# Half of the gate projections made between the attention blocks and kept in DRAM, and eight modulation chunks moved from the merge to the MLP

## The chip, the cores and the metric

The kernel runs on one core of one Trainium2 chip. The time is that of one execution on the device, in microseconds; of runs of one kernel the median is taken. Profiles are of one execution. A core has TensorE (matrix products, in the profile PE, its weight loads PEld), VectorE (DVE), ScalarE (ACT), GpSimd (POOL) and SyncE (SP, which here only issues DMAs).

## The reference

Two layers of a trunk are run over 640 tokens: 512 latent ones and 128 of context. Cut to what matters here, a layer is

```python
h = modulate(rms_norm(x, g_attn), sh1, sc1)          # sh1 ... gt2: six pieces of silu(c) @ w_mod + b_mod
cb, cc, cv, gq, gk, gv, nq, nk, nv, mq, mkv, mkr, gates = in_project(h, w_in)
y_conv, y_gqa, y_na, y_mla = ...                     # a short convolution and three kinds of attention
g1, g2, g3, g4 = split(sigmoid(gates), 4)            # each 1024 wide
merged = (g1 * (y_conv @ w_branch_conv) + g2 * (y_gqa @ w_branch_gqa)
          + g3 * (y_na @ w_branch_na) + g4 * (y_mla @ w_branch_mla))
x = x + gt1 * (merged @ w_o)
x = x + gt2 * (square(relu(modulate(rms_norm(x, g_mlp), sh2, sc2) @ w_ff1)) @ w_ff2)
```

The `gates` depend on `h` alone, not on the attention. `c` is one vector for the latent tokens and another for the context tokens, so the modulation is 6 x 1024 columns for each of two vectors.

## The kernel before

Activations lie with their features on the partitions: a chunk is 128 features x 640 tokens, two halves of 320. A weight slab is 128 output columns with all its row chunks, mostly 8: 128 x 1024 numbers, 512 KB. For precision each operand is split into a high and a low part in fp32r (`prefetch`, `split`): ScalarE casts the high part, VectorE subtracts it to get the low part. A product is then three matmuls per row chunk (`steps`, L199 to L201: high x high, high x low, low x high), and a slab of 8 row chunks is 48 matmuls of 320 columns, 24 per half. One such group of three is called a step.

`plan` lists all slabs in the order of use (`feed`). `take` hands out the next one and, through `look`, splits the following one meanwhile. A large slab (tag `w`) has two buffers for the raw weights and two for each part. A small slab (tag `b`: the branch projections `wb` of 2 or 4 row chunks, and the MLA heads' second projections) has one of each, and `look` never splits one small slab while another is being used:

```python
            if last == "b" and (self.raws[0][3] if self.raws else self.feed[0][3]) == "b":
                return
```

A layer has three stages.

*Mixers* (`mixers`, `attend`). 16 heads of 5 blocks each (four of latent queries, one of context queries) go through a software pipeline: scores on TensorE, minimum on VectorE, exponential on ScalarE, a factor on GpSimd, transposition on TensorE (L538), split, product with the values. 8 heads are of windowed attention (GQA), 4 of neighbourhood attention, 4 of latent attention (MLA). Between the parts of a block `fill` runs steps of the remaining projections on TensorE: a list of tasks in a fixed order, with a budget per block (`RATE`, in units in which a step is 410). A task may wait until so many heads have begun or ended (`wait`); `fill` then returns with nothing done, whatever stands behind that task, and its budget adds up. TensorE's order is the program's; the order on the other engines in this stage is a scheduler's. Two banks of PSUM are there for projections.

*Merge* (`merge`). For each of eight output columns j and each of the four branches: the gate's slab (`wg`, large) times `h`, the branch's small slab (`wb`) times the branch's output, tanh of the gate on ScalarE (L889), the product (L891, L893) on VectorE, the sum over branches on GpSimd. At the end of a column `mh` and `ml` are the split sum (L902, L903). A column is 252 matmuls. From here to the end of the MLP the order of every engine is that of the program, SP's too. In layer 0's merge 32 modulation chunks are made beside it (`mod_chunk`): a chunk is 128 columns of the modulation, one DMA of 512 KB into `wm`, which has one buffer, and two passes of VectorE over it (L253), one for each vector. There are five places for chunks in each column from the second on.

*MLP* (`mlp`, `boundary`). Up and down projections in four quarters, each slab large. In layer 0 the 48 chunks of the next layer's modulation are made there, one per slab in 54 places; what is left would be made in one piece before the last `boundary`.

Of the kernel before, what the change touches and what calls it, by code (L numbers as in the profile page):

```python
# [17 lines left out]
P = 128  # L18
D = 1024
KC = D // P  # L20
DEPTH = 2
# [18 lines left out]
HEAD = 100  # L40
FILL_SLABS = (GQ + 1, GQ + 2, CONV + 2, CONV + 4, CONV, GQ + 3, NQC, NK, NV, MKV, NQC + 1, NK + 1, NV + 1,
              MQ, MQ + 1, MKR, HEAD, HEAD + 1, CONV + 3, HEAD + 2, CONV + 5, HEAD + 3, CONV + 1)
# gate, first row chunk and number of chunks of its branch's projection; first chunk of y
BRANCHES = ((1, 0, 4), (2, 4, 2), (0, 8, 2), (3, 6, 2))
Y_OF = {0: 0, 1: 2, 2: 6, 3: 8}
# [20 lines left out]
class Net:  # L66
    def __init__(self, ctx, nc, tc, t):
# [7 lines left out]
        self.ydram = [self.dr.tile([10, P, NTOK], F32, name=f"ydram{l}") for l in range(DEPTH)]  # L75
        self.xdram = self.dr.tile([P, KC, NTOK], F32, name="xdram")
# [19 lines left out]
    def psum(self, n1, n2=0):  # L96
        """PSUM for one phase: n1 single banks, n2 pairs of banks"""
# [18 lines left out]
    def plan(self, l):  # L116
        t, f = self.t, self.feed
        wa = lambda c: f.append((t["wa"][l, c], KC, P, "w", True))
        for c in (GK, GQ, GV) + FILL_SLABS:
            if c == MKR:  # L120
                f.append((t["wkr"][l], KC, 32, "w", True))
            elif c >= HEAD:
                f.append((t["wmla"][l, c - HEAD], 1, 384, "b", True))
            else:
                wa(c)
        for j in range(KC):
            for g, c0, n in BRANCHES:
                f.append((t["wg"][l, j, g], KC, P, "w", False))
# [11 lines left out]
    def raw(self):  # L140
        """start the load of the next slab"""
# [5 lines left out]
    def prefetch(self, dst=None):  # L147
        """split the next slab; start the load of the one after it"""
# [9 lines left out]
        if eng and kc == KC:  # L158
            # in halves, so that no engine is held for long
# [1373 lines left out]
```

## Time and profile before

| | |
|---|---|
| time, three runs | 2405.25, 2408.97, 2410.58 us (median 2408.97) |
| profiled execution | span 2405.3 us from the first to the last instruction |
| TensorE | busy 2315.2 us (96%), mean granted clock 0.987 |
| VectorE, ScalarE, GpSimd | 1404.0, 935.7, 367.3 us (58, 39, 15%) |
| DMA | 242.96 MB, 101 GB/s in the mean |
| mixers of layer 0, layer 1 | 84.4 to 405.2, 1261.3 to 1579.0 us |
| first merge, its eight columns | 405.2 to 701.2 us |

Busy time is the union of an engine's instructions. A matmul is shown with some 310 ns though 1012 of them start in 148 us: each is pipelined into the next, so TensorE's busy share says that it was never left waiting for long, not that it ran at its peak. The start of one block and the start of the next tell more.

### The profile page before, as it was taken

Reading aid. Unit: us, or ns where it says so; the run is one execution under the profiler, and the core shown is the slowest. Engines: PE = TensorE matmul, PEld = TensorE weight load, DVE = VectorE, ACT = ScalarE, POOL = GpSimd, SP = SyncE. Lnnn points to the kernel's source line nnn. Section 1 sums busy time; section 2 is a strip of 40 time slices with the busy share of each in tenths; the row PEclk is TensorE's granted clock in tenths of the full one; section 3 lists DMA queues with packets and bytes.
Section 4 is the critical chain, followed back from the end, with each engine's and each line's share of the span. In section 5 each row is a group of like instructions: output and inputs, shape, how many; then the busy total and the mean of one; then the engine's idle time right before and its main releaser. Section 6 shows DMA issues by size and latency. Waiting matters only on the chain. (4 is left out here: it accounts for less than half of the span.)

```text
span 2405.3 us, 39685 instructions
## 1 busy us (share of the span) xinstructions
PE 2315.2 (96%) x15766; PEld 2251.6 (94%) x15766; DVE 1404.0 (58%) x2744; ACT 935.7 (39%) x1877; POOL 367.3 (15%) x468
## 2 busy tenths in 40 slices
PE   8899888999999999999999998999999999999998
PEld 4899888999999999999988997899999999999998
DVE  5776676666645777776467767753333454343433
ACT  5555554322224332222255656542222343131311
POOL 0333321111111000000123333211111200000001
PEclk9999999999999999999999999999999999999999
DMA  6323312444431344443331231042222212222222
GB/s 231 96 72 86 91 35 102 167 142 148 151 114 59 132 158 157 147 153 123 97 124 58 83 112 38 25 162 73 82 71 86 90 45 72 78 76 75 79 80 71
DMA packets 85321, 242.96 MB, mean 101 GB/s; under 512 B 9744, under 2 KB 31248, under 8 KB 83728
## 3 DMA queue, kind: packets, MB, share of 16 engines
q1 hardware_dynamic: 85136, 240.43, 30.9%
q8 instruction: 124, 2.03, 0.3%
q14 instruction: 61, 0.50, 0.1%
HBM read 222.14 MB, written 12.75 MB: 98 GB/s over the span
## 5 line engine op out<-in xcount | busy, mean ns | idle before, releaser
L199 PE MATMUL pr<-hhi,whiw 128*128 128x320 f32 (+1 forms) x2752 | 868.4, 316 | 20.5 <-ACT st L300 9.6
L201 PE MATMUL pr<-hhi,wlow 128*128 128x320 f32 (+1 forms) x2752 | 852.7, 310 | 2.3 <-DVE wlow L166 1.4
L200 PE MATMUL pr<-hlo,whiw 128*128 128x320 f32 (+1 forms) x2752 | 853.4, 310 | 0.1
L199 PEld LDWEIGHTS pr<-hhi,whiw 128*128 128x128 f32 (+1 forms) x2752 | 516.4, 188 | 26.9 <-ACT st L300 11.7
L201 PEld LDWEIGHTS pr<-hhi,wlow 128*128 128x128 f32 (+1 forms) x2752 | 515.6, 187 | 5.0 <-DVE wlow L166 2.6
L200 PEld LDWEIGHTS pr<-hlo,whiw 128*128 128x128 f32 (+1 forms) x2752 | 516.7, 188 | 3.4 <-DVE hlo L1159 2.6
L165 ACT CAST whiw<-raww 128x1024 fp32r<-128x1024 f32 x184 | 192.7, 1047 | 286.6 <-PE pr L200 269.4
L166 DVE TENSOR_TENSOR wlow<-raww,whiw 128x1024 fp32r<-128x1024 f32 x184 | 237.1, 1289 | 60.8 <-ACT whiw L165 60.3
L199 PE MATMUL pr<-hh,whiw 128*128 128x320 f32 x832 | 257.0, 309 | 0.0
L200 PE MATMUL pr<-hl,whiw 128*128 128x320 f32 x832 | 256.9, 309 | 0.0
L201 PE MATMUL pr<-hh,wlow 128*128 128x320 f32 x832 | 256.9, 309 | 0.0
L253 DVE SCALAR_TENSOR_TENSOR junk<-wm,cb 128x1024 bf16<-128x1024 f32 x160 | 195.7, 1223 | 46.8 <-DMA wm<-in_wm 43.9
L916 DVE SCALAR_TENSOR_TENSOR x<-pr,mod,x 128x256 f32<-128x256 f32 x320 | 107.7, 379 | 195.1 <-PE pr L201 192.9
L1114 POOL TENSOR_TENSOR sqs<-sqs,sq 128x320 f32<-128x320 f32 x48 | 47.7, 993 | 969.8 <-ACT sq L1112 941.9
L529 POOL TENSOR_SCALAR p<-p,sm 128x512 f32<-128x512 f32 (+3 forms) x160 | 123.2, 771 | 369.5 <-DVE sm L528 299.6
L894 POOL TENSOR_TENSOR acc<-acc,sg 128x320 f32<-128x320 f32 x96 | 89.0, 931 | 521.1 <-DVE sg L893 521.0
L524 ACT ACTIVATE p<-S,sm 128x641 f32<-128x641 f32 (+6 forms) x160 | 112.1, 701 | 139.0 <-DVE sm L515 65.1
L889 ACT ACTIVATE sg<-pr 128x320 f32<-128x320 f32 x128 | 55.5, 437 | 284.1 <-PE pr L201 276.3
L200 PEld LDWEIGHTS pr<-hl,whiw 128*128 128x128 f32 x832 | 156.4, 188 | 0.0
L199 PEld LDWEIGHTS pr<-hh,whiw 128*128 128x128 f32 x832 | 156.4, 188 | 0.0
L201 PEld LDWEIGHTS pr<-hh,wlow 128*128 128x128 f32 x832 | 156.4, 188 | 0.0
L893 DVE SCALAR_TENSOR_TENSOR sg<-sg,pr 128x320 f32<-128x320 f32 x96 | 46.2, 487 | 187.4 <-PE pr L201 187.4
(207 smaller groups left out, 3774.5 us busy)
## 6 DMA issues: line engine op xcount, KB each, us to landing
raww<-in_w SPq DMA_DIRECT2D x128, 512.0 KB, 3.6
wm<-in_wm SPq DMA_DIRECT2D x80, 512.0 KB, 3.7
raww<-in_wg SPq DMA_DIRECT2D x64, 512.0 KB, 3.8
raww<-in_wa SPq DMA_DIRECT2D x42, 512.0 KB, 3.6
wm<-in_wm SPq DMA_DIRECT2D x8, 1024.0 KB, 14.3
raww<-in_wo SPq DMA_DIRECT2D x16, 512.0 KB, 3.6
rawb<-in_wb SPq DMA_DIRECT2D x48, 128.0 KB, 2.1
kt<-kt SPq DMA_DIRECT2D x24, 224.0 KB, 3.2
```

The source lines that it names most:

```text
L165: nc.scalar.copy(hi, raw)
L166: nc.vector.tensor_tensor(lo, raw, _r(hi), ALU.subtract)
L199: nc.tensor.matmul(out, lhsT=whi[:, kw, :], rhs=xhi[:, kx, sl], start=(i == 0), stop=False)
L200: nc.tensor.matmul(out, lhsT=whi[:, kw, :], rhs=xlo[:, kx, sl], start=False, stop=False)
L201: nc.tensor.matmul(out, lhsT=wlo[:, kw, :], rhs=xhi[:, kx, sl], start=False, stop=(i == n - 1))
L253: nc.vector.scalar_tensor_tensor(self.junk, raw, 1.0, self.cb[v], ALU.mult, ALU.mult, accum_out=self.mod[l]["mod"][:, v, i:i + 1])
L524: nc.scalar.activation(p[:, :B["n"]], B["sc"], AF.Exp, bias=sm[:, 0:1], scale=-1.0, accum_out=sm[:, 1:2])
L529: nc.gpsimd.tensor_scalar(p[:, :n], p[:, :n], sm[:, 1:2], 1.0, ALU.mult, ALU.mult)
L889: nc.scalar.activation(sg, gp[hf][:, :HALF], AF.Tanh, scale=0.5)
L894: nc.gpsimd.tensor_tensor(a, a, sg, ALU.add)
L916: self.nc.vector.scalar_tensor_tensor(x[:, j, o + a:o + b], ps[:, a:b], m[:, v, g0 + j:g0 + j + 1], x[:, j, o + a:o + b], ALU.mult, ALU.add)
L1114: eng.tensor_tensor(self.acc[h], self.acc[h], sq, ALU.add)
```

## The change

Sixteen of the 32 gate slabs of a layer, those of columns 4 to 7 (`EARLY`), are made in the mixers, as sixteen more fill tasks between the others (`None` in the table `FILL`, of which two of its eight lines are shown). Each passes its tanh through a tile `gt` to DRAM (`gdram`). The budgets per block are raised. In the merge, columns 4 to 7 have only the branches' small slabs; the tanh values come back by DMA, four tiles at the end of column 2 into the last chunks of `mh` and `ml`, twelve into the tiles of `h` once the last gate of column 3 has been made. Layer 0's merge makes 24 chunks, two per branch in columns 1 to 3, and the other eight stand at the head of the MLP's list.

```diff
+EARLY = tuple(range(4, KC))
+EARLY_GATES = tuple((j, b[0]) for j in EARLY for b in BRANCHES)
+FILL = (("q1", (GQ + 1,)), ("q2", (GQ + 2,)), None, ("c0", (CONV + 2, CONV + 4, CONV)), ("q3", (GQ + 3,)), None,
+        ("nq0", (NQC,)), None, ("nk0", (NK,)), ("nv0", (NV,)), None, ("ckv", (MKV,)), None, ("nq1", (NQC + 1,)),
...
-RATE = (2000, 2200, 2000)
+RATE = (3500, 3700, 3500)
...
+    def early_gate(self, l, n):
+        w = self.take()
+        t = self.at.tile([P, NTOK], F32, name="gt", tag="gt", bufs=1)
+        for h in range(2):
+            ps = self.bank()
+            yield from self.steps(ps[:, :HALF], w, self.h, hsl(h))
+            self.nc.scalar.activation(t[:, hsl(h)], ps[:, :HALF], AF.Tanh, scale=0.5)
+        self.nc.sync.dma_start(self.gdram[l][n], t)
...
     def merge(self, l, x):
-        self.mod_todo = deque([(0, i) for i in range(16, 48)] if l == 0 else [])
+        self.mod_todo = deque([(0, i) for i in range(16, 40)] if l == 0 else [])
...
             for j in range(KC):
                 for i, (g, c0, n) in enumerate(BRANCHES):
-                    w = self.take()
-                    if j:
-                        self.mod_chunk()
-                    gp = [self.half(w, h, hf) for hf in range(2)]
+                    if j not in EARLY:
+                        w = self.take()
+                        if j:
+                            self.mod_chunk()
+                            self.mod_load()
+                        gp = [self.half(w, h, hf) for hf in range(2)]
+                        if (j, i) == (EARLY[0] - 1, len(BRANCHES) - 1):
+                            for name in ("hhi", "hlo"):
+                                u = self.hp.tile([P, KC, NTOK], F32R, name=name, tag=name)
+                                early.extend(_r(u[:, k]) for k in range(KC))
+                            gates(4, len(EARLY_GATES))
...
                     w = self.take()
-                    if j and i == 0:
-                        self.mod_load()
-                        self.mod_chunk()
...
                     for hf in range(2):
...
+                        if j in EARLY:
+                            tg = early[(j - EARLY[0]) * len(BRANCHES) + i][:, hsl(hf)]
+                        else:
+                            tg = sg
+                            nc.scalar.activation(sg, gp[hf][:, :HALF], AF.Tanh, scale=0.5)
...
-                    if j:
+                    if j and j not in EARLY:
+                        self.mod_chunk()
                         self.mod_load()
...
     def mlp(self, l, x, first):
-        self.mod_todo = deque([(l + 1, i) for i in range(48)] if l + 1 < DEPTH else [])
+        self.mod_todo = deque([(0, i) for i in range(40, 48)] + [(1, i) for i in range(48)] if l == 0 else [])
```

Three places where the order of instructions changes. In these rows `S` is a pair of PSUM banks, `pr` one bank, `hhi` and `hlo` the two parts of `h`, `whiw` and `wlow` those of a large slab, `whib` and `wlob` those of a small one.

TensorE in layer 0's mixers, the seventh head's second block, before: from one transposition of probabilities (L538) to the next.

```order
L538 MATMUL S_2209<-ident,p 128x128 x5
L199 MATMUL pr<-hhi,whiw 128x320
L200 MATMUL pr<-hlo,whiw 128x320
L201 MATMUL pr<-hhi,wlow 128x320
...
L479 MATMUL S_2228<-kt,qt 128x128
L480 MATMUL S_2228<-kt,qt 128x128
...
L538 MATMUL S_2246<-ident,p 128x128 x5
```

The same place now (lines are shifted by 15).

```order
L553 MATMUL S_2659<-ident,p 128x128 x5
L494 MATMUL S_2666<-kt,qt 128x128
L495 MATMUL S_2666<-kt,qt 128x128
L570 MATMUL pr<-pt,vt 128x128 x2
L553 MATMUL S_2686<-ident,p 128x128 x5
```

Where five steps stood between two transpositions, none stands now. In the blocks before it there are 8 or 9 steps instead of 5, and in the neighbourhood heads' second block 76 in one piece.

VectorE in layer 0's merge, the second branch of a column, before: the low parts of a small and a large slab, a chunk (`junk`, two passes), the branch's product (`sg`).

```order
L166 TENSOR_TENSOR wlob<-rawb,whib 128x256 [waits DMAHW1_49,Activation_49]
L166 TENSOR_TENSOR wlow<-raww,whiw 128x1024 [waits DMAHW2_49,Activation_49]
L253 SCALAR_TENSOR_TENSOR junk,mod_106<-wm,cb_4589 128x1024 [waits DMAHW4_49,DVE_49]
L253 SCALAR_TENSOR_TENSOR junk,mod_106<-wm,cb_4590 128x1024 [waits DVE_49]
L893 SCALAR_TENSOR_TENSOR sg<-sg,pr 128x320 [waits PE_49,Activation_49] x2
L166 TENSOR_TENSOR wlob<-rawb,whib 128x256 [waits DMAHW5_49,Activation_49]
```

A branch of columns 1 to 3 now.

```order
L181 TENSOR_TENSOR wlob<-rawb,whib 128x256 [waits DMAHW4_49,Activation_49]
L181 TENSOR_TENSOR wlow<-raww,whiw 128x1024 [waits DMAHW5_49,Activation_49]
L268 SCALAR_TENSOR_TENSOR junk,mod_108<-wm,cb_5583 128x1024 [waits DMAHW7_49,DVE_49]
L268 SCALAR_TENSOR_TENSOR junk,mod_108<-wm,cb_5584 128x1024 [waits DVE_49]
L941 SCALAR_TENSOR_TENSOR sg<-sg,pr 128x320 [waits PE_49,Activation_49] x2
L268 SCALAR_TENSOR_TENSOR junk,mod_108<-wm,cb_5583 128x1024 [waits DMAHW2_49,DVE_49]
L268 SCALAR_TENSOR_TENSOR junk,mod_108<-wm,cb_5584 128x1024 [waits DVE_49]
L181 TENSOR_TENSOR wlob<-rawb,whib 128x256 [waits DMAHW0_49,Activation_49]
```

A second chunk stands behind the product, ahead of the next branch's low parts.

VectorE in the merge's columns 4 to 7, now, from the end of column 5 on: the split sum (`ml`), then low parts of small slabs and products by turns, each product with a gate from `hhi`.

```order
L954 SCALAR_TENSOR_TENSOR ml<-acc,mh 128x640 [waits Activation_49]
L181 TENSOR_TENSOR wlob<-rawb,whib 128x512 [waits DMAHW0_49,Activation_49]
L939 SCALAR_TENSOR_TENSOR acc<-hhi,pr 128x320 [waits PE_49] x2
L181 TENSOR_TENSOR wlob<-rawb,whib 128x256 [waits DMAHW1_49,Activation_49]
L941 SCALAR_TENSOR_TENSOR sg<-hhi,pr 128x320 [waits PE_49] x2
```

Before, a large slab's low part and a chunk stood between a small slab's low part and its product, and the next small slab's low part came behind the next gate's slab. Now each small slab's low part stands directly behind the product of the small slab before it.

## Rows read from the trace of the kernel before

**Rows 1.** Windows; columns: stretch, PE, PEld, DVE, ACT, POOL busy (x instructions), PEclk, DMA, GB/s
```profile
84.39:405.21 320.82, 291.40 (x2045) 275.45 (x2043) 234.35 (x533) 185.29 (x438) 103.57 (x151) 0.97 0.20 60
405.21:553.20 147.99, 146.42 (x987) 144.88 (x988) 94.65 (x151) 46.33 (x82) 20.45 (x22) 1.00 0.54 178
553.20:701.20 148.00, 148.00 (x1012) 148.00 (x1011) 89.44 (x136) 39.00 (x68) 22.18 (x24) 1.00 0.44 139
701.20:1237.40 536.20, 533.89 (x3639) 530.94 (x3638) 354.75 (x667) 177.72 (x309) 29.36 (x28) 1.00 0.37 125
1261.33:1579.00 317.67, 290.49 (x2045) 274.30 (x2042) 234.00 (x532) 185.72 (x438) 103.70 (x151) 0.97 0.20 61
```

**Rows 2.** Timeline of PE, block starts; columns: start, us, engine, line, operation, tiles, count
```profile
159.19 0.63 PE L538 MATMUL S<-ident,p 128*128 128x128 f32 x4 [0.99 <-DVE pt L545]
...
167.56 0.71 PE L538 MATMUL S<-ident,p 128*128 128x128 f32 x5
...
177.90 0.49 PE L538 MATMUL S<-ident,p 128*128 128x128 f32 x3
...
183.79 0.38 PE L538 MATMUL S<-ident,p 128*128 128x128 f32 x2
```

**Rows 3.** Timeline of PE, blocks at the end of the first mixers
```profile
392.61 0.82 PE L538 MATMUL S<-ident,p 128*128 128x128 f32 x6
...
397.99 1.06 PE L538 MATMUL S<-ident,p 128*128 128x128 f32 x6 [1.32 <-issue]
```

**Rows 4.** Windows of 10 us in the first mixers and merge
```profile
290.00:300.00 10.00, 6.34 (x42) 4.95 (x40) 9.29 (x19) 5.93 (x16) 5.77 (x14) 1.00 0.01 2
340.00:350.00 10.00, 8.86 (x46) 8.44 (x47) 6.56 (x12) 4.74 (x10) 2.05 (x2) 0.66 0.00 0
410.00:420.00 10.00, 9.10 (x59) 8.35 (x58) 5.53 (x8) 5.86 (x10) 0.00 (x0) 1.00 1.04 393
```

**Rows 5.** Timeline of DVE, first chunks of the first merge
```profile
453.33 1.22 DVE L253 SCALAR_TENSOR_TENSOR junk<-wm,cb 128x1024 bf16<-128x1024 f32 x1
...
459.54 1.23 DVE L253 SCALAR_TENSOR_TENSOR junk<-wm,cb 128x1024 bf16<-128x1024 f32 x1 [3.72 <-DMA wm<-in_wm]
...
471.94 1.23 DVE L253 SCALAR_TENSOR_TENSOR junk<-wm,cb 128x1024 bf16<-128x1024 f32 x1 [0.22 <-DMA wm<-in_wm]
```

**Rows 6.** Timeline of DVE at the end of a merge column
```profile
482.67 0.49 DVE L893 SCALAR_TENSOR_TENSOR sg<-sg,pr 128x320 f32<-128x320 f32 x1 [0.39 <-PE pr L201]
484.92 0.82 DVE L903 SCALAR_TENSOR_TENSOR ml<-acc,mh 128x640 fp32r<-128x640 f32 x1 [1.75 <-ACT mh L902]
485.66 0.69 DVE L166 TENSOR_TENSOR wlob<-rawb,whib 128x512 fp32r<-128x512 f32 x1
```

**Rows 7.** Lines by form, first merge: columns as the page's part 5
```profile
L889 ACT ACTIVATE sg<-pr 128x320 f32<-128x320 f32 x63 | 27.3, 437 | 133.8 <-PE pr L201 126.0 <-DVE acc L891 7.5 <-POOL acc L894 0.3
...
L165 ACT CAST whib<-rawb 128x256 fp32r<-128x256 f32 x24 | 9.7, 406 | 44.4 <-PE pr L200 38.9 <-DMA rawb<-in_wb 5.5
...
L166 DVE TENSOR_TENSOR wlob<-rawb,whib 128x256 fp32r<-128x256 f32 x24 | 13.9, 577 | 0.0
```

**Rows 8.** DMA issues, whole run: out<-in, engine, count, KB, us to landing
```profile
rawb<-in_wb SPq DMA_DIRECT2D x48, 128.0 KB, 2.1
...
rawb<-in_wb SPq DMA_DIRECT2D x16, 256.0 KB, 2.7
```

**Rows 9.** DMA issues from 405.8 to 416.7 us
```profile
x<-ydram SPq DMA_DIRECT2D x8, 320.0 KB, 6.9
...
rawb<-in_wb SPq DMA_DIRECT2D x1, 128.0 KB, 6.3
```

**Rows 10.** Timeline of DVE around the last MLP boundary of layer 0
```profile
1163.29 0.68 DVE L916 SCALAR_TENSOR_TENSOR x<-pr,mod,x 128x256 f32<-128x256 f32 x2 [2.84 <-PE pr L201]
...
1164.48 1.22 DVE L166 TENSOR_TENSOR wlow<-raww,whiw 128x1024 fp32r<-128x1024 f32 x1
```

More of the change, by code (lines that the diff above doesn't have):

```diff
@@ L75, in __init__ @@
         self.ydram = [self.dr.tile([10, P, NTOK], F32, name=f"ydram{l}") for l in range(DEPTH)]
+        self.gdram = [self.dr.tile([len(EARLY_GATES), P, NTOK], F32, name=f"gdram{l}") for l in range(DEPTH)]
         self.xdram = self.dr.tile([P, KC, NTOK], F32, name="xdram")
@@ L118, in plan @@
         wa = lambda c: f.append((t["wa"][l, c], KC, P, "w", True))
-        for c in (GK, GQ, GV) + FILL_SLABS:
-            if c == MKR:
+        gates = iter(EARLY_GATES)
+        slabs = [GK, GQ, GV]
+        for task in FILL:
+            slabs += task[1] if task else [GATE]
+        for c in slabs:
+            if c == GATE:
+                f.append((t["wg"][l][next(gates)], KC, P, "w", True))
+            elif c == MKR:
                 f.append((t["wkr"][l], KC, 32, "w", True))
@@ L711, in part @@
                     yield ns
-            tasks = [gqa_q(1), gqa_q(2), ("c0", (ns for ns in self.conv(l, 0) if ns >= 0)), gqa_q(3),
-                     na_q(0), na_k(0), na_v(0), ("ckv", M.keys()), na_q(1), na_k(1), na_v(1), ("mq", M.queries()),
-                     ("kr", M.rotary()), ("m0", M.prep(0)), ("m1", M.prep(1)), ("c1", part()), ("m2", M.prep(2)),
-                     ("c2", part()), ("m3", M.prep(3)), ("c3", part())]
+            gen = {"c0": (ns for ns in self.conv(l, 0) if ns >= 0), "ckv": M.keys(), "mq": M.queries(), "kr": M.rotary()}
+            gen.update(gqa_q(c) for c in (1, 2, 3))
+            for c in range(2):
+                gen.update((na_q(c), na_k(c), na_v(c)))
+            gen.update((f"m{hd}", M.prep(hd)) for hd in range(4))
+            gen.update((f"c{i}", part()) for i in (1, 2, 3))
+            gates = iter(range(len(EARLY_GATES)))
+            tasks = []
+            for task in FILL:
+                if task:
+                    tasks.append((task[0], gen[task[0]]))
+                else:
+                    n = next(gates)
+                    tasks.append((f"g{n}", self.early_gate(l, n)))
+            assert next(gates, None) is None
             names = [n for n, _ in tasks]
@@ L855, in merge, with gates @@
             order = [Y_OF[g] + q for g, _, n in BRANCHES for q in range(n)]
-            raw = {}
-            for i, c in enumerate(order):
-                raw[c] = x[:, i] if i < KC else yp.tile([P, NTOK], F32, name="acc", tag="acc", bufs=3)
-                if i < BRANCHES[0][2]:
-                    nc.sync.dma_start(raw[c], self.ydram[l][c])
+            raw = {c: x[:, i] if i < KC else _r((mh, ml)[i - KC][:, KC - 1]) for i, c in enumerate(order)}
+            for c in order[:BRANCHES[0][2]]:
+                nc.sync.dma_start(raw[c], self.ydram[l][c])
+            early = deque(_r(a[:, k]) for k in (KC - 1, KC - 2) for a in (mh, ml))
+            def gates(a, b):
+                for n in range(a, b):
+                    nc.sync.dma_start(early[n], self.gdram[l][n])
             for j in range(KC):
-                acc = None
+                acc = yp.tile([P, NTOK], F32, name="acc", tag="acc", bufs=3)
                 for i, (g, c0, n) in enumerate(BRANCHES):
-                    w = self.take()
-                    if j:
-                        self.mod_chunk()
-                    gp = [self.half(w, h, hf) for hf in range(2)]
                     yc = Y_OF[g]
+                    if j not in EARLY:
+                        w = self.take()
[8 more added lines that the diff above has]
+                            gates(4, len(EARLY_GATES))
                     for q in range(n if j == 0 else 0):
                         self.split(yh[:, yc + q], yl[:, yc + q], raw[yc + q])
-                    if acc is None:
-                        acc = yp.tile([P, NTOK], F32, name="acc", tag="acc", bufs=3)
                     w = self.take()
-                    if j and i == 0:
-                        self.mod_load()
-                        self.mod_chunk()
                     if (j, i) == (0, 0):
@@ L901, in merge @@
                             self.silu(yp, a, D)
+                elif j == EARLY[0] - 2:
+                    gates(0, 4)
                 nc.scalar.activation(mh[:, j], acc, AF.Copy, scale=0.5)
@@ L906, in merge @@
                 self.mod_chunk()
-            self.mod_done(0, 16, 48)
+            self.mod_done(0, 16, 40)
         wop = s.enter_context(tc.tile_pool(name="wop", bufs=1, side="right", reuse_waits="tile"))
@@ L995, in mlp @@
             up(q)
+            if l == 0 and q == 1:
+                self.mod_done(0, 40, 48)
             down(q - 1)
```

19 lines of the change are left out of this document (11 added, 8 removed).

## The prediction

> **What bounds the kernel now.** I read the windows by stage first, then block starts on TensorE inside the mixers, then VectorE and the DMA issues in the merge, because the change takes from one stage and gives to the other. The windows [rows 1] show the split. In the first merge TensorE is busy for 146.4 us of 148.0 and then for all of 148.0; 1012 matmuls in 148.0 us are 146 ns each, and I take that as the pace of a 128x320 matmul. The MLP is the same: 533.9 of 536.2. So there a stage costs its matmuls. The mixers are another matter: 29.4 of 320.8 us idle in layer 0, 27.2 of 317.7 in layer 1. The busy count flatters them, as a matmul's tail covers short gaps. The starts of the blocks show what is lost [rows 2]: the fifth head takes 18.71 us (159.19 to 177.90) with 22 fill steps, while the five blocks from 167.56 to 183.79 take 16.23 with 21 steps, without a gap. A step is three matmuls, 0.44 us, so a dense head is 7.0 us of attention plus its steps, and the fifth head loses 18.71 - 7.0 - 9.7 = 2.0 us. Added up over all 79 block starts of a layer, against the dense pace, it is 47 us; 94 us for both layers is the most that better filling could give.
>
> **The change, part by part.** The matmuls are the same, 14,382 rows on TensorE in both. Per layer 16 gate slabs of 48 matmuls, 16 x 48 x 0.146 = 112 us, leave the merge and enter the mixers: nothing by itself. What counts is the waiting in either place.
>
> *Mixers.* The first six heads get 38 steps instead of 22. That is 7.0 + 16.7 = 23.7 us of TensorE per head, while the other engines needed at most the 18.7 us that a head takes now. Their 2.0 us each should go: -12 us per layer. But the fill stops whenever its next task waits for a head, and the gates behind that task wait with it. The order shows that from the seventh head on there are 23 blocks of 78 without a step, where there were 11. A block without steps takes 2.7 us: (397.99 - 392.61) / 2 [rows 3], though TensorE needs about 1.4 of it (7.0 / 5). Nineteen such blocks before the tail cost 19 x 1.3 = 25 us; the same stretch loses 47 - 12 - 5 (tail, as before) = 30 now, most of it in the MLA preparations, and I let 8 of that stand since gate steps follow them now. Sum: -12 + 25 + 8 - 30 = -9; the half clock that shows where steps are missing (0.66 from 340 to 350 us) [rows 4] takes some back: I take -4 per layer, -8 in all. Bounds: -94 and +50 (19 blocks a layer at 4 us). The sixteen casts, tanh and stores a layer go to engines busy for 234, 185 and 104 us of 321 [rows 1], so they cost nothing there; without that cover the 32 tanh alone would be 14 us a layer (0.44 each) [rows 7].
>
> *Modulation chunks, layer 0.* A chunk is two VectorE passes over a 512 KB tile with one buffer: its load starts when the last chunk has been read. Chunks in a row start at 453.33, 459.54 and, two later, at 471.94: 6.2 us each, with 3.72 us waiting for the load [rows 5]. Before, there are 32 in seven columns; now 24 in columns 1 to 3, two per branch. VectorE runs in order, so the chain is 23 x 6.2 + 2.5 = 145 us from 453.3 to 598.4, then 1.5 us for `ml` and the next low part (0.82, 0.69) [rows 6]: 599.9. TensorE would be through column 3 at 553.2 (four columns of 252 matmuls in 148.0 us from 405.2) [rows 1]. Every gate needs its low part from that same VectorE queue, so it waits: +46 us. Without the load wait it would be 0 (24 x 2.5 = 60 us, under 111); with loads slowed to 4.5 us, 65.
>
> *Columns 4 to 7, both layers.* Only the small branch slabs are left, and these have one raw and one split buffer and no large slab between them to work ahead under. So each runs in series. From low part to low part between two 128x256 slabs: load 2.1 us [rows 8], cast 0.41, low part 0.58 [rows 7], some 0.2 for hand-overs, 3.3 us, for 12 matmuls of 1.75. From a 128x512 slab to the next: 24 matmuls are 3.5 us, 0.3 of it before the low part is needed, then 0.39 until VectorE sees the end [rows 6], 0.49 for the product queued ahead, 0.58: 4.7. Into the next column VectorE has the longest queue: from the end of the matmuls to the end of the new low part it is 485.66 + 0.69 - 482.28 = 4.1 us [rows 6], 5.5 with the matmuls. A column is 4.7 + 3.3 + 3.3 + 5.5 = 16.8 us against 60 x 0.146 = 8.8: +8.0. Four columns are 32; the last transition falls away (-3), and the second slab waits behind the twelve gate tiles which SP issues just ahead of it (+3). That burst is 3.93 MB; at the 393 GB/s of a full queue [rows 4] it is 10 us, and a small load behind four 320 KB tiles landed after 6.3 us instead of 2.1 [rows 9, 8]. Layer 0: +32, as the chain already covers its entry. Layer 1 also waits at the entry, 4.1 - 0.3: +36. Bounds per column: 7 with no load wait, 15 at half clock.
>
> *MLP of layer 0.* There are 54 places for chunks and now 56 chunks, so two run in one piece before the last boundary, ahead of the low part that TensorE needs. Now that low part ends at 1165.7, 2.4 us after the matmuls' results are read [rows 10], hidden under 3.5 us of products. With 2.5 + 3.7 + 2.5 in front it is 8.7 later: about +8. The other six have free places; without those they would cost 6.2 each.
>
> **Sum.** -8 + 46 + 32 + 36 + 8 = +114 us on the profiled span of 2405.3: 2519. That execution is at the low end of the runs (2405.25 to 2410.58, median 2408.97), so with the median's 3.7 us I say 2523.
>
> **Rivals.**
> *Filling closes every gap* (chance 0.14). For it: 38 steps a head are more than any head lost. Against: 23 blocks have none. The mixers give -94 instead of -8: 2437.
> *Faster* (0.05). The same full cover, and small slabs that keep pace: merge and MLP cost 46 + 32 + 36 + 8 = 122 now, so it decides when the small columns cost less than 40 for both layers, 5 a column instead of 8, a step of about 2.5 us. Then 2405 and less; I put it at 2400. Against it stands the load of 2.1 us in series with two passes of 1.0.
> *Half clock in the small columns* (0.12). The granted clock averaged 0.66 in a stretch with 46 matmuls in 10 us, two thirds of it at 1.2 GHz after attention without steps, but stayed at 1.00, 2.4 GHz, in one with 42 [rows 4]; so it can go either way at 36 in 10 us. Matmuls at twice the length make the steps 4.4, 7.9 and 7.0: 23.7 a column, +55 over eight columns, half of that likely: 2550. The Trainium skill, "TensorE: Matmul & The Clock Gate", section "Loop structure matters more than you think", says that a loop which waits for a DMA between every group of matmuls lets TensorE go cold. By that rule the small columns would run wholly at half clock, 2578; the trace here shows both.
> *Bare blocks cost double* (0.06). VectorE's put-off work lands on blocks without steps, 4 us each: +50, 2573.
> *The change as forecast*: 0.63.
>
> **Range and chances.** The forecast's own spread is 2490 to 2550 (a small step of 2.9 to 3.7 us, a chunk of 6.0 to 6.5, mixers by 15 either way). Reaching to full cover in part and half clock in part, 2455 to 2562 holds 8 in 10. About 0.2% (5 us) is what a measurement tells from no change. Slower 0.93, no change 0.02, faster 0.05.
>
> **What would show it.** In the profile after: chunks 6.2 us apart on VectorE for 145 us in layer 0's merge, and TensorE idle there for some 45 us, waiting for low parts; after it, small slabs 3.3 to 5.5 us apart with TensorE about half busy, in both layers; the first of these behind a burst of twelve loads; heads 1 to 6 at 23 to 24 us without idle time, and then blocks of 2.7 us with 76 steps in one piece. It is wrong if chunks come closer than 5 us, if small slabs follow at 1.75 to 2.5 us, or if the mixers end more than 40 us earlier than 113 us beyond their time now.

## The result and the profile after

The changed kernel takes 2573.56 us (median of 2568.64, 2572.73, 2574.38 and 2575.16), the kernel before 2407.16 beside it: 1.0694 times as long, 95% interval 1.0676 to 1.0711. The forecast was 2523 with a range to 2562; the direction was right, the size 50 us short.

Stage windows of the changed kernel come first; columns as in [rows 1]. In their order: the mixers of layer 0 from the first block on, its merge, its output projection with the MLP up to layer 1's first block, and the same three of layer 1.

```profile
89.31:531.89 442.58, 407.05 (x2780) 390.52 (x2778) 243.83 (x548) 215.71 (x499) 121.08 (x165) 0.96 0.23 74
531.89:802.56 270.67, 216.71 (x1249) 204.33 (x1249) 139.21 (x237) 56.77 (x103) 39.89 (x46) 0.89 0.42 144
802.56:1375.95 573.39, 557.58 (x3768) 552.85 (x3768) 395.69 (x733) 191.70 (x341) 41.26 (x37) 0.99 0.38 133
1375.95:1818.52 442.57, 407.03 (x2780) 390.29 (x2778) 243.79 (x548) 215.58 (x499) 121.26 (x165) 0.96 0.23 74
1818.52:2041.57 223.05, 196.81 (x1249) 188.11 (x1249) 79.09 (x125) 53.09 (x95) 41.28 (x46) 0.97 0.33 112
2041.57:2572.60 531.03, 519.04 (x3530) 516.17 (x3528) 231.72 (x431) 160.87 (x269) 24.64 (x26) 0.99 0.23 75
```

The mixers of before are in [rows 1] (layer 1's are cut off 0.4 us short there); its other stages, cut at the same places:

```profile
405.21:704.08 298.87, 297.30 (x2016) 295.76 (x2017) 184.58 (x288) 85.77 (x151) 42.67 (x47) 1.00 0.49 157
704.08:1261.33 557.25, 550.30 (x3737) 546.30 (x3735) 372.02 (x694) 190.93 (x339) 38.20 (x35) 1.00 0.38 128
1579.40:1875.61 296.21, 296.09 (x2016) 295.68 (x2017) 99.48 (x144) 81.85 (x143) 42.68 (x47) 1.00 0.30 97
1875.61:2405.30 529.69, 518.63 (x3530) 515.93 (x3528) 230.24 (x429) 160.95 (x269) 24.63 (x26) 0.99 0.24 74
```

With the 112 us of moved matmuls taken off the mixers and added to the merge, the spans compare as below. (The larger budgets also run 11 more steps, 4.9 us, ahead of each layer's first block; these are counted with the mixers. Over the whole run both profiles show 15,766 matmuls.)

| stage | forecast | measured |
|---|---|---|
| mixers, both layers | -8 | +32 |
| merge of layer 0 (chunks 46, small columns 32) | +78 | +84 (43 and 41) |
| merge of layer 1 | +36 | +39 |
| MLP of layer 0 | +8 | +11 |
| MLP of layer 1 | 0 | +1 |
| sum | +114 | +167 |

Of the 53 us that are missing, 40 belong to the mixers and 9 to layer 0's small columns (the first four columns of that merge took 190.6 us instead of 148.0, which leaves 41 of the 84 for the others). The other terms hold within 3 us, and their steps can be read off the trace.

*The chunks* (answer to [rows 5]). VectorE's timeline in layer 0's merge:

```profile
585.11 1.22 DVE L268 SCALAR_TENSOR_TENSOR junk<-wm,cb 128x1024 bf16<-128x1024 f32 x1 [2.78 <-DMA wm<-in_wm]
...
591.22 1.23 DVE L268 SCALAR_TENSOR_TENSOR junk<-wm,cb 128x1024 bf16<-128x1024 f32 x1 [2.14 <-DMA wm<-in_wm]
...
597.44 1.23 DVE L268 SCALAR_TENSOR_TENSOR junk<-wm,cb 128x1024 bf16<-128x1024 f32 x1 [2.92 <-DMA wm<-in_wm]
```

Chunks start 6.1 and 6.2 us apart, each behind its own load; the chain of 24 lasts from 579.0 to 725.2, 146 us where 145 was said.

*The small columns.* VectorE's timeline in layer 1's column 6, from the low part of its first small slab to that of the next column (the passes between the low parts are left out):

```profile
2010.55 0.68 DVE L181 TENSOR_TENSOR wlob<-rawb,whib 128x512 fp32r<-128x512 f32 x1
...
2015.23 0.42 DVE L181 TENSOR_TENSOR wlob<-rawb,whib 128x256 fp32r<-128x256 f32 x1
...
2018.26 0.94 DVE L181 TENSOR_TENSOR wlob<-rawb,whib 128x256 fp32r<-128x256 f32 x1 [0.29 <-ACT whib L180]
...
2021.81 1.01 DVE L181 TENSOR_TENSOR wlob<-rawb,whib 128x256 fp32r<-128x256 f32 x1 [0.22 <-ACT whib L180]
...
2027.68 0.69 DVE L181 TENSOR_TENSOR wlob<-rawb,whib 128x512 fp32r<-128x512 f32 x1
```

The steps are 4.68, 3.03, 3.55 and 5.87 us, forecast 4.7, 3.3, 3.3 and 5.5: 17.1 for a column instead of 16.8. This column had its granted clock at 1.00 from end to end; layer 0's columns 5 and 6, at 0.90 and 0.84, took 18.7 and 20.3 (more on that at the extra matmuls below).

*The mixers* lost time where they were to gain it. Windows: the first blocks without steps, the start of the piece of 76 steps, and two MLA preparations in one piece.

```profile
247.40:263.70 16.30, 11.72 (x70) 10.40 (x68) 13.35 (x39) 11.13 (x28) 5.44 (x7) 0.79 0.22 69
279.20:289.20 10.00, 8.56 (x49) 8.37 (x50) 5.58 (x15) 4.79 (x12) 1.89 (x3) 0.83 0.60 167
358.40:379.80 21.40, 17.41 (x96) 16.04 (x97) 10.74 (x24) 7.79 (x19) 3.78 (x4) 0.84 0.18 58
428.20:453.90 25.70, 22.12 (x123) 20.50 (x124) 10.61 (x20) 9.15 (x22) 4.51 (x9) 0.80 0.07 24
```

In the last two TensorE starts 96 matmuls in 21.4 us and 123 in 25.7, where dense 128x320 work starts 146 in 21.4; and each of the four has part of its time at 1.2 GHz. Two of TensorE's waits in the third window, for a split by VectorE (L229) and for a readout by ScalarE (L315):

```profile
PE pr L1436 <- DVE kt L229: 1.6, 1, 1.6
PE pr L1404 <- ACT st L315: 1.5, 1, 1.5
```

To say what is lost, I take from the time between two block starts its matmuls, each at the median start-to-start time of its shape over the run (0.147 us for 128x320). Layer 0, in us:

| blocks | before | the forecast's account | after |
|---|---|---|---|
| heads 1 to 6 | 12.4 | 0 | 12.1 |
| 19 blocks without steps | | 25 | 17 |
| the other blocks up to the fifteenth head | 31.5 | 8 | 28 |
| tail | 4.3 | 5 | 4 |
| sum | 48 | 38, taken as 43 | 61 |

### The profile page after: what moved, and what is told of

The parts are those of the page before. It is cut to its first block, busy times and chain, and to the rows that moved or that the text cites. A ratio compares the mean times of both kernels' runs of the same rounds, so it can differ in the third digit from the quotient of the medians.

```text
span 2572.6 us, 39887 instructions
## 1 busy us (share of the span) xinstructions
PE 2381.0 (93%) x15766; PEld 2295.2 (89%) x15766; DVE 1385.3 (54%) x2746; ACT 939.5 (37%) x1909; POOL 404.3 (16%) x500
## 4 chain that ended last, share of the span: by engine, by line
PE 76%; DVE 8%; DMA 7%; ACT 4%; issue 3%; POOL 1%; SPq 0%; DVEq 0%; ACTq 0%
PE pr L214 22%; PE pr L216 22%; PE pr L215 22%; DMA wm<-in_wm 4%; PE pr L570 3%; PE S L553 2%; DMA rawb<-in_wb 2%; DVE junk L268 1%; ACT p L539 1%; PE S L494 1%; PE S L495 1%; PE pr L289 1%; DVE wlob L181 1%; DVE kt L229 1%; DVE pt L560 1%
## 5 line engine op out<-in xcount | busy, mean ns | idle before, releaser
L214 PEld LDWEIGHTS pr<-hhi,whiw 128*128 128x128 f32 (+1 forms) x2752 | 522.0, 190 | 19.7 <-DVE kt L229 4.2
L216 PEld LDWEIGHTS pr<-hhi,wlow 128*128 128x128 f32 (+1 forms) x2752 | 520.9, 189 | 4.8 <-DVE wlow L181 2.6
L215 PEld LDWEIGHTS pr<-hlo,whiw 128*128 128x128 f32 (+1 forms) x2752 | 522.0, 190 | 3.6 <-DVE hlo L1212 2.6
L180 ACT CAST whiw<-raww 128x1024 fp32r<-128x1024 f32 x152 | 159.2, 1047 | 290.3 <-PE pr L215 266.6
L181 DVE TENSOR_TENSOR wlow<-raww,whiw 128x1024 fp32r<-128x1024 f32 x152 | 188.9, 1243 | 56.6 <-ACT whiw L180 56.3
L214 PE MATMUL pr<-yh,whib 128*128 128x320 f32 x320 | 112.8, 353 | 49.8 <-ACT whib L180 49.7
L178 POOL TENSOR_TENSOR wlow<-raww,whiw 128x512 fp32r<-128x512 f32 (+1 forms) x76 | 97.4, 1282 | 322.0 <-ACT whiw L177 287.1
```

The costliest lines, as they stand in the source:

```text
L178: e.tensor_tensor(lo[:, c], raw[:, c], _r(hi[:, c]), ALU.subtract)
L180: nc.scalar.copy(hi, raw)
L181: nc.vector.tensor_tensor(lo, raw, _r(hi), ALU.subtract)
L214: nc.tensor.matmul(out, lhsT=whi[:, kw, :], rhs=xhi[:, kx, sl], start=(i == 0), stop=False)
L215: nc.tensor.matmul(out, lhsT=whi[:, kw, :], rhs=xlo[:, kx, sl], start=False, stop=False)
L216: nc.tensor.matmul(out, lhsT=wlo[:, kw, :], rhs=xhi[:, kx, sl], start=False, stop=(i == n - 1))
```

## The experiments

All twelve are edits of the changed kernel; times are medians, and the kernel before took 2403 to 2405 us beside them.

| | us | over before, 95% interval |
|---|---|---|
| second buffer for chunks | 2533.3 | 1.0524 to 1.0555 |
| second buffers for small slabs | 2517.7 | 1.0458 to 1.0489 |
| extra matmuls in the small columns | 2573.9 | 1.0693 to 1.0725 |
| gates spread in the fill list | 2521.6 | 1.0467 to 1.0502 |
| the three edits | 2425.4 | 1.0072 to 1.0102 |
| the three, 27 chunks | 2421.7 | 1.0052 to 1.0085 |
| gate tiles by fours | 2569.8 | 1.0670 to 1.0708 |
| half the gates, edits as above | 2430.5 | 1.0095 to 1.0125 |
| put-off work at 900 | 2569.9 | 1.0673 to 1.0708 |
| put-off work at 2200 | 2578.4 | 1.0712 to 1.0741 |
| the three, 27 chunks, 900, by fours | 2418.7 | 1.0048 to 1.0076 |
| gate halves read by VectorE, 900 | 2569.1 | 1.0675 to 1.0711 |

**A second buffer for the chunks**, in space that only the merge uses (the sum's tile `acc` gives up one of its three buffers for it, and the two layers share one tile of scales):

```diff
-        if self.mod_todo and self.wm is None:
+        while self.mod_todo and len(self.wm) < self.wm_ahead:      # 2 in the merge
...
-            raw = self.xp.tile([P, D], F32, name="wm", tag="wm", bufs=1)
+            raw = (self.yp.tile([P, D], F32, name="wm2", tag="wm2") if odd else
+                   self.xp.tile([P, D], F32, name="wm", tag="wm"))
```

> Against the changed kernel (2573.6 us). Chunk tiles of layer 0's merge get a second buffer, nothing else changes there. Theory A (a chunk waits for its own load, 3.7 us, because the one buffer is read to the end first): the 24 chunks no longer come 6.2 us apart but fit under the 37 us of a column, columns 2 to 4 start 37 us apart instead of 44 to 52, and the kernel takes 2531 us (-42). Theory B (it is VectorE's two passes and its queue that hold the column, not the load): chunks still about 6 us apart, 2570 to 2576. Theory C (as A, and the half clock behind the chain goes as well): 2523.

2533.3, theory A. Window of the four full columns:

```profile
526.80:680.50 153.70, 148.88 (x1008) 147.86 (x1008) 115.79 (x187) 47.04 (x84) 29.74 (x24) 1.00 0.63 212
```

The 1008 matmuls that took 191 us in the changed kernel (531.9 to 722.5) take 154. VectorE makes the same 48 passes, so it was the load and not the passes.

**Second buffers for the small slabs** of columns 4 to 7. To make room, `acc` gives up a buffer and the last four gate tiles come two columns later, so the burst at the entry is eight tiles instead of twelve:

```diff
+        alt = self.alt if tag == "b" and self.alt_n % 2 else None
...
-            if last == "b" and (self.raws[0][3] if self.raws else self.feed[0][3]) == "b":
+            if last == "b" and (self.raws[0][3] if self.raws else self.feed[0][3]) == "b" and (
+                    self.alt is None or self.ready):
                 return
```

> Against the changed kernel (2573.6 us). The small branch slabs of columns 4 to 7 get a second raw and a second split buffer, so that a slab is loaded and split while the one before is multiplied; the last four gate tiles are loaded two columns later. Theory A (load, cast and low part in series make these columns slow, +39 us over their matmuls in either layer): a column falls to about 9 to 10 us, 2503 us (-70). Theory B (TensorE at half clock is a cause of its own there): a column stays at 13 or more, 2540. Theory C (the burst of gate tiles holds the loads): only the first of the four columns stays slow, about 20 us, 2520.

2517.7, between A and B. The windows of the four small columns, layer 0 (in which column 3 still ends late, behind the chunks) and layer 1:

```profile
716.90:767.40 50.50, 42.94 (x240) 40.09 (x240) 28.81 (x56) 10.65 (x22) 20.18 (x22) 0.86 0.50 160
1938.40:1983.80 45.40, 39.59 (x240) 36.83 (x240) 25.14 (x50) 10.67 (x22) 20.15 (x22) 0.96 0.48 155
```

Four columns took 80 and 72 us and now take 50 and 45, against 35 of matmuls. The series of load, cast and low part is most of it; the smaller burst can have brought some of the 3 us a layer that it is worth (below). What is left is at the entry (below).

**Extra matmuls** behind each small slab's own, so that TensorE is busy while it waits:

```diff
+                    if j in EARLY:
+                        ps = self.bank()
+                        for q in range(6):
+                            nc.tensor.matmul(ps[:, :HALF], lhsT=yh[:, 0, :P], rhs=yh[:, 0, hsl(0)], start=(q == 0), stop=(q == 5))
```

> Against the changed kernel (2573.6 us). Behind each small slab's matmuls in columns 4 to 7 TensorE makes six more 128x320 matmuls into a bank that nobody reads (0.9 us a slab, 14 us a layer), in the time in which it now waits; all results stay. Theory A (part of the miss in these columns is half clock: they take 80 us in layer 0 and 72 in layer 1, where 64 were forecast): the granted clock there goes to 1.00 and the columns to about 64 each, 2551 us (-23). Theory B (the steps are set by load and passes, whatever the clock): within 5 us of 2574. Theory C (the extra matmuls stand in the way): 2580 to 2600.

2573.9, theory B's time. Layer 1's columns 4 and 6, first in the changed kernel, then with the extra matmuls:

```profile
1970.00:1992.00 22.00, 14.42 (x60) 12.52 (x60) 6.37 (x14) 2.46 (x5) 5.41 (x6) 0.77 0.44 162
2010.30:2027.50 17.20, 11.00 (x61) 8.90 (x61) 7.68 (x14) 2.46 (x5) 5.13 (x6) 1.00 0.13 39
```

```profile
1969.50:1991.20 21.70, 16.43 (x85) 15.38 (x85) 6.42 (x14) 2.46 (x5) 5.45 (x6) 0.84 0.44 159
2008.40:2025.50 17.10, 13.84 (x84) 12.31 (x84) 7.57 (x14) 2.47 (x5) 5.18 (x6) 1.00 0.14 39
```

The granted clock rises (0.77 to 0.84; in column 5 from 0.91 to 1.00), the columns hardly move: 71.6 us for the four become 71.0, and layer 0's go from 80.1 to 77.7, the extra matmuls' own time included.

That does not make half clock free. The clock rose mostly in the steps that wait for loads. The first step of a column is another matter: ScalarE's cast of the second slab waits there until TensorE has done with the one split buffer (5.9 us in layer 0's column 5, 4.4 in layer 1's column 6), so that 24 matmuls stand in the series, as in the forecast's own account of this step. The first steps of layer 0's columns 5 and 6 and of layer 1's column 6 in the changed kernel, then of layer 0's columns 5 and 6 with the extra matmuls:

```profile
748.73:754.95 6.22, 5.48 (x25) 4.96 (x24) 1.58 (x5) 0.41 (x1) 0.00 (x0) 0.73 0.07 21
767.38:774.55 7.17, 6.77 (x25) 6.11 (x25) 1.58 (x5) 0.40 (x1) 0.00 (x0) 0.56 0.06 18
2010.55:2015.23 4.68, 3.94 (x25) 3.42 (x24) 1.58 (x5) 0.41 (x1) 0.00 (x0) 1.00 0.10 28
```

```profile
750.22:756.43 6.21, 5.82 (x29) 5.55 (x29) 1.57 (x4) 0.41 (x1) 0.00 (x0) 0.73 0.07 21
768.88:774.79 5.91, 5.64 (x29) 5.25 (x29) 1.58 (x4) 0.41 (x1) 0.00 (x0) 0.71 0.09 25
```

The step takes 4.68 us at 1.00, about 6 at 0.71 to 0.73 and 7.2 at 0.56. Where the extra matmuls lifted the clock in it, it shrank: from 5.87 to 4.68 in layer 1's column 5 and from 5.83 to 4.68 in layer 0's column 7, both at 1.00 then. The other three steps of a column hardly change: in layer 0's column 4 they took 14.0 us at 0.76 and take 13.5 at 1.00. So theory B holds for these and fails for the first step. Added up over the first steps of the eight columns, half clock cost some 9 us (an estimate from the steps above 4.68 us, with 1.5 for each column 4 from the run with gate tiles by fours).

**The gates spread in the fill list**: one wherever the task behind it would still wait for a head.

```diff
-FILL = (("q1", (GQ + 1,)), ("q2", (GQ + 2,)), None, ("c0", (CONV + 2, CONV + 4, CONV)), ("q3", (GQ + 3,)), None,
...
+FILL = (('q1', (1,)), ('q2', (2,)), ('c0', (17, 19, 15)), ('q3', (3,)), ('nq0', (6,)), ('nk0', (8,)), ('nv0', (10,)),
+        None, None, None, ('ckv', (14,)), None, None, ('nq1', (7,)), None, None, None, None, ('nk1', (9,)),
...
```

> Against the changed kernel (2573.6 us). Only the order of the fill list changes: a gate stands wherever the task behind it would still be waiting for a head, so that every head from the first to the fourteenth has 38 steps, instead of 38 in six heads and 23 blocks with none. Theory A (the mixers' miss is the blocks without steps and the pieces in which their work comes later): a mixer stage falls from 442.6 us to about 396, 2482 us (-92). Theory B (only the blocks without steps and the 76 steps in one piece cost; the MLA preparations lose their 8 us each wherever they stand): 427 a stage, 2542. Theory C (VectorE or ScalarE can't keep 38 steps a head going in the neighbourhood and MLA heads): 435 or more, 2560.

2521.6, between A and B. The two mixer stages:

```profile
90.37:508.96 418.59, 397.26 (x2781) 383.74 (x2778) 250.34 (x548) 215.49 (x499) 122.47 (x165) 0.97 0.24 78
1354.82:1770.43 415.61, 392.34 (x2781) 379.08 (x2778) 249.13 (x548) 215.26 (x499) 122.10 (x165) 0.99 0.25 79
```

24 and 27 us less for the same matmuls: 51 in all, more than the 40 by which the term was off. By the account above, layer 0 loses 38 us: 7.3 in heads 1 to 6, 26.6 from there to the fifteenth head, 4.2 in the tail. Blocks 31 to 42 went from 14.0 to 1.3, so the blocks without steps are mended. The MLA preparations are not: blocks 51 to 63 still lose 16.0 (24.4 in the changed kernel, 15.7 before), 10 of them in one block, where TensorE waits 3.2 us for a cast of ScalarE and then three times 0.6 to 0.7 inside the preparation, at half clock for a part of it.

**The three edits together**:

> The three edits together on the changed kernel: second buffer for the chunks (2533.3 alone), second buffers for the small slabs (2517.7 alone), gates spread in the fill list (2521.6 alone). Theory A (three separate causes, the gains add up: 40 + 56 + 52 us off 2573.6): 2425 us, still slower than the kernel before (2404). Theory B (they share waiting time, chiefly at the entry to column 4): 2440 or more. Theory C (with the waits gone the half clock goes too): 2410 or less.

2425.4, theory A: the three gains add up within the runs' spread of 4 to 7 us, so the causes share little. What is left in layer 1's small columns is told by TensorE's waits there (us in total, times, longest) and by SP's timeline:

```profile
PE pr L223 <- ACT whib L187: 5.6, 3, 4.6
```

```profile
1838.73 4.35 SPq L913 DMA_DIRECT2D hhi<-gdram  x8
1843.17 0.49 SPq L165 DMA_DIRECT2D rawb<-in_wb  x1
```

Eight gate tiles are issued ahead of the second small slab, and its cast comes 4.6 us too late.

**27 chunks in the merge**, a third one in one branch of columns 1 to 3, so that none is left over in the MLP:

> As the three edits together, and 27 instead of 24 chunks in layer 0's merge (a third one in one branch of columns 1 to 3), so that the MLP has 53 chunks for its 54 places and none runs in a piece before its last boundary. Theory A (the two chunks left over cost the MLP of layer 0 its 8 to 11 us): 9 us less than the three edits together, and the wait of the product behind the MLP's last low part is gone. Theory B (that MLP lost its time elsewhere): no difference beyond 2 us. Theory C (the merge can't take three more): more time than the three edits.

2421.7. The wait before the MLP's last boundary is there with the three edits and gone here:

```profile
PE pr L225 <- DVE wlow L188: 8.2, 1, 8.2
```

From the end of the output projection to layer 1's first block it is 502.4 us instead of 512.2 (-9.8, theory A). Only 3.8 of that show in the medians and none in the two profiled spans: layer 0's merge is 2.1 longer (theory C in part), and the rest is spread over mixers and output projection, where two profiles of one code differ by as much.

**Gate tiles by fours**, each group a column ahead:

```diff
-                            gates(4, len(EARLY_GATES))
+                            gates(4, 8)
...
                     gates(0, 4)
+                elif EARLY[0] <= j < KC - 2:
+                    gates(4 * (j - 2), 4 * (j - 1))
```

> The changed kernel, but the gate tiles of columns 5 to 7 are loaded four at a time, each group a column ahead, instead of twelve at once at the entry to column 4. Theory A (as forecast, the second small slab waits some 3 us behind the burst): 2568 us (-6 in both layers). Theory B (the first of the four columns is slow because of the burst, 22 to 26 us against 17 to 20): 2558 (-8 a layer). Theory C (the burst is hidden; that column is slow since its slabs are in series like the others'): within 3 us of 2573.6.

2569.8: -3.8 in the medians, with overlapping intervals, but -6.4 in the profiled spans, and the place shows theory A: in column 4 the first step took 8.82 and 9.45 us (layer 0, layer 1) and takes 6.17 and 6.21. The forecast's 3 us for the burst was right; what still stands above column 6's 4.68 goes with the clock, which was 0.67 and 0.73 in these steps. VectorE in layer 1, here:

```profile
1966.42 0.68 DVE L181 TENSOR_TENSOR wlob<-rawb,whib 128x512 fp32r<-128x512 f32 x1
...
1972.63 0.42 DVE L181 TENSOR_TENSOR wlob<-rawb,whib 128x256 fp32r<-128x256 f32 x1
```

**Half the gates early**, columns 6 and 7 only, with 30 steps a head (`RATE = (2750, 2950, 2750)`), 30 chunks in columns 1 to 5, and the two buffer edits:

> Only columns 6 and 7 get their gates early (8 gates a layer instead of 16), spread in the fill list at 30 steps a head; 30 chunks of layer 0 in the merge's columns 1 to 5 with a second buffer, the small slabs with second buffers. Theory A (what the mixers gain by an even fill is kept, about 9 us a layer, and two small columns cost about 4): 2394 us, faster than before (2404). Theory B (the mixers' waits belong to particular blocks and not to the number of steps: no gain there): 2404 to 2415. Theory C: 2420 or more.

2430.5, theory C, a miss of 36 us. Its mixers:

```profile
85.24:461.29 376.05, 345.06 (x2411) 329.82 (x2409) 241.22 (x539) 200.25 (x466) 115.23 (x158) 0.96 0.22 70
```

Less the 56 us of eight gates that is 320.0, the 320.8 of before [rows 1]: nothing gained by an even 30 steps a head; merge and output projection cost 9 us a layer on top, the same sum in both layers. Heads 1 to 6 lose 12.2 us with 30 steps, 12.4 with 22 (before), 12.1 with 38 (changed kernel), 7.3 with 38 in the other order. The number of steps alone does not set this loss; the order of the list, which differs between these runs, counts as well.

**What does**: the put-off work, handed out in other portions.

```diff
-            self.drain(1300)
+            self.drain(900)
```

> The changed kernel (2573.6 us) with the put-off work of VectorE and ScalarE handed out at 900 instead of 1300 a block, so that the two halves of a query or key pair fall into two blocks and not into one. Theory A (the first six heads still lose 12 us with 38 steps because TensorE meets such lumps: 4.4 us in one block behind two key splits, 3.6 in another behind two query splits): those blocks lose 1 us or less, the six heads some 6 us instead of 12, 2560 us. Theory B (the waits come from the readout of the last projection's bank, which is in the queue in any case): same losses, 2570 to 2577.

2569.9, within the spread of the changed kernel's own runs; but the six heads lose 8.6 instead of 12.1. TensorE's waits from 188 to 199 us, the fifth head's first block, in the changed kernel and with smaller portions:

```profile
PE pr L570 <- DVE y L593: 2.6, 1, 2.6
```

```profile
PE pr L570 <- DVE y L593: 0.8, 1, 0.8
```

The product with the values waits for a bank that VectorE reads out only behind two key splits (1.08 and 1.46 us). VectorE in the changed kernel (a pass between the splits is left out):

```profile
189.09 1.08 DVE L229 TENSOR_TENSOR kt<-st,kt 64x896 fp32r<-64x896 f32 x1
...
190.62 1.46 DVE L229 TENSOR_TENSOR kt<-st,kt 64x896 fp32r<-64x896 f32 x1 [0.38 <-ACT kt L228]
192.11 0.42 DVE L593 TENSOR_TENSOR y<-pr,plo 64x256 f32<-64x256 f32 x1
```

With one split a block the block's loss falls from 4.4 to 1.1: theory A there. The third head's third block keeps its 3.6: theory B there. So each theory holds for one of the two blocks.

> The changed kernel (2573.6 us) with the put-off work handed out at 2200 instead of 1300 a block. Theory A (lumps are what TensorE meets): more and larger waits in the six filled heads, 16 us and more there, 2580 us or more. Theory B (as above, the readout alone): 2570 to 2577.

With 2200 in the same line: 2578.4 (+4.8), but the six heads lose 12.1 as before: theory A said 16. Two halves came together already at 1300. The time went elsewhere: in the profile the mixers are 0.3 and 0.8 us longer than in the changed kernel and the two merges, which the edit does not touch, 2.5 and 3.9. In layer 1's merge the first steps of columns 6 and 7 take 6.88 and 5.87 us at a granted clock of 0.59 and 0.71, instead of 4.68 at 1.00, which is 3.4 of the 3.9; the runs with a second chunk buffer and with put-off work at 900 had half clock in the same two steps. So that part is the clock's change from run to run, and the total decides for neither theory.

**Gate halves read by VectorE**, for the block that was left:

```diff
-            self.nc.scalar.activation(t[:, hsl(h)], ps[:, :HALF], AF.Tanh, scale=0.5)
+            self.nc.vector.tensor_scalar(t[:, hsl(h)], ps[:, :HALF], 1.0, 0.0, ALU.mult, ALU.add)
+            self.nc.scalar.activation(t[:, hsl(h)], t[:, hsl(h)], AF.Tanh, scale=0.5)
```

> The changed kernel with put-off work at 900 a block (2569.9 us), and the early gates' halves read from their bank by VectorE, ScalarE making the tanh in place afterwards. It asks what is left of the filled heads' waits, 3.6 us in the third head's third block, where TensorE waits for a bank until ScalarE makes a tanh that stands in its queue behind a softmax. Theory A (the readout's place in ScalarE's queue is the cause): that block loses 2 us or less, the kernel takes 2564 us (-3 a layer). Theory B (VectorE is as late there, since the softmax waits for it): that block still loses over 3 us, 2567 to 2573. Theory C (32 more passes of 0.44 us a layer on VectorE cost elsewhere): 2576 or more.

2569.1, in B's range and no different from 2569.9 given the spread, but the block shows A: its loss falls from 3.6 to 0.9. TensorE's wait there, in the changed kernel and now:

```profile
PE pr L570 <- ACT gt L875: 1.8, 1, 1.8
```

```profile
PE pr L570 <- DVE gt L875: 0.6, 1, 0.6
```

The gain is given back: the first head's third block now loses 2.1, blocks 51 to 63 lose 26.7 instead of 24.7.

**All that helped together**, the gate tiles behind the loads of the next two small slabs:

> The three edits with 27 chunks (2421.7 us), put-off work at 900 a block, and the gate tiles four at a time behind the loads of the next two small slabs. The wait for the second small slab behind eight gate tiles (4.6 us a layer in the three edits) should go, and about 3 us a layer of the filled heads. Theory A (all of it shows): 2406 us, even with the kernel before (2404). Theory B (lumps are not a cause): 2412. Theory C (no gain): 2420.

2418.7 (2412.13 to 2420.3; the profiled execution was the shortest), nearest to C and still 0.5 to 0.8% slower than before. One of the two gains came: TensorE's longest wait in layer 1's small columns falls from 4.6 to 1.1 us. The other did not: with the gates spread, the first six heads lose the same at 900 as at 1300, block for block. Its merges are 197.4 and 193.7 us, where their matmuls would take 187 and 184 at the pace of before. No version here beats the kernel before.

## Why the prediction was wrong

The chunk chain, the small columns, the burst and the two chunks left over were right in mechanism, and near in size: 122 us forecast, 135 measured, counting the MLP of layer 1. Nine of the 13 are layer 0's small columns, 41 instead of 32, in large part because their first steps ran at half clock. What these waits are made of is shown by taking them away (-40, -56, -9.8 in its stage).

The step that failed is the sum of the mixers, "-12 + 25 + 8 - 30 = -9", taken as -4 a layer; it was +16 a layer. It has three parts.

- "Their 2.0 us each should go": they stayed, 12.4 to 12.1. That the sums agree is chance, since they are made of other blocks: the second head's first two blocks lost 2.1 and 1.6 us before and 0.3 and 0 now, as forecast, while the third head's third went from 1.5 to 3.6 and the fifth head's first from 2.0 to 4.4. I had reasoned that 23.7 us of TensorE a head covers what the other engines need in 18.7. But the loss is not a matter of mean load. It sits in a few blocks where TensorE wants a bank that another engine reads late, because that engine has a lump of put-off work or stands behind a softmax. The runs at 22, 30 and 38 steps lose the same, and moving the lump or the readout moves the loss (4.4 to 1.1, 3.6 to 0.9). In these blocks more steps do not help, since the waiting product stands ahead of the next steps on TensorE; with the same 38 steps in another order the six heads lost 7.3.
- "I let 8 of that stand since gate steps follow them now": 28 stood. The gates stood in the list behind the preparations, not beside them: these came in one piece of up to 39 matmuls and 20 steps, and TensorE waited inside the piece for readouts and splits of what it had just made (1.5 and 1.6 us in one such piece). Spreading the gates brought 24 and 27 us a layer back, in all three parts.
- "Nineteen such blocks before the tail cost 19 x 1.3 = 25": the nineteen are there, at 17 us.

Of the rivals, half clock in the small columns was to add 27 to 55 us. The clock did fall there, to 0.67 in layer 0's column 4, and cost some 9 us by the first steps of the columns; the run with extra matmuls (2573.9) raised it to 1.00 in two of those six that were below. By the Trainium skill, "TensorE: Matmul & The Clock Gate", section "Loop structure matters more than you think", a long DMA wait between matmuls lets TensorE go cold; the prediction's sentence said it of any wait for a load. The trace agrees in layer 1's column 4, where TensorE waited 3.7 us for a slab whose load came late and the granted clock was 0.50 from 1979.66 to 1983.00 us. In its column 6, at waits of up to 0.8 us for a slab and 2.9 at the entry, the clock stayed at 1.00, and in column 5 it fell behind the same 2.9 us, which are no wait for a load. Bare blocks at double price fell (17 us, not 50): that its 2573 is the measured time is chance. Full cover fell (61 us lost, not 0). The result lay outside the range because I gave the mixers 15 us either way over both layers when both ends of that term, -94 and +50, had been worked out: +32 lies inside them.

## What to carry to other kernels

Filler work helps a stage only where the waits lie: before counting on it, list the blocks that lose time, name for each what TensorE waits for, and ask whether more filler comes ahead of the waiting instruction or behind it. Work moved out of a stage that was bound by its matmuls takes away cover, too: here small loads in series had been hidden by the large slabs, and a one-buffer load chain by their length. The first three mends added up, but six of them only led back to 0.6% above the start.

## What was not expected of the hardware

- A granted clock that counts in one step of four: the first step of a small column took 4.68 us at 1.00 and 7.17 at 0.56, while the others, which wait for loads, took 14.0 us at 0.76 and 13.5 at 1.00. Which first steps fell to half clock changed from run to run of much the same code.
- Waits cost more than their length. In the mixers of layer 0, counting a start that comes late by up to 1.25 times the matmul's own time as slow and the rest of the loss as gaps, the changed kernel loses 36 us in gaps and 25 to slow starts (before 29 and 19; with the gates spread 18 and 20). After its wait of 3.2 us the spread version starts 128x320 matmuls every 0.27 us instead of 0.147, from 347.3 to 352.3 us, at a granted clock of 0.50.
- VectorE's pass over a chunk took 1329 ns in the mean with the second chunk buffer and 1225 in the changed kernel. The median is 1225 in both: nine of the 48 passes took 1.76 to 1.78 us, and each of the nine began while GpSimd was at its second addition of a branch (the two took 2.7 us instead of 1.8). The pass ahead of it, which lay wholly within the additions, took 1.25. In the changed kernel no pass met an addition. One of the nine, GpSimd first, then VectorE:

```profile
584.94 2.70 POOL L949 TENSOR_TENSOR acc<-acc,sg 128x320 f32<-128x320 f32 x2 [18.74 <-DVE sg L948]
```

```profile
585.65 1.25 DVE L273 SCALAR_TENSOR_TENSOR junk<-wm,cb 128x1024 bf16<-128x1024 f32 x1
...
586.94 1.78 DVE L273 SCALAR_TENSOR_TENSOR junk<-wm,cb 128x1024 bf16<-128x1024 f32 x1
```
